# Parameter arithmetic queued where its inputs are ready, squares and PSUM evacuations with priority, in a one-core decoder layer

## The chip, the cores and the metric

The kernel runs on one core of one Trainium2 chip. The metric is the device time of one execution in microseconds (us), lower being better. A profile of one execution shows the engines of that core: PE (TensorE, the matrix engine), DVE (VectorE), ACT (ScalarE), POOL (GpSimd) and SP (SyncE, which here only issues DMAs). Each engine works through a queue of its own in a fixed order; an instruction that waits holds up everything behind it in its queue.

## The reference

One layer of a hybrid decoder, on 256 prompt tokens and 8 x 8 sample tokens (320 token columns in all):

```
h    = rms_norm(x, norm_mix)
proj = h @ w_in                        # split into S5 input u and retention q, k, v, g
S5:  dt = exp(log_step); lam_bar = exp(lam*dt); b_bar = (lam_bar - 1)/lam * b
     x_t = lam_bar * x_(t-1) + b_bar u_t;  y = Re(C x) + d*u;  gelu, sigmoid GLU
retention, 8 heads: rotary(q), rotary(k); masked decayed q k^T v + q R; group norm; silu(g)*o
x = x + concat(s5, ret) @ w_out
x = x + (silu(gate) * up) @ w_ffn_out,  gate, up = rms_norm(x, norm_ffn) @ w_ffn_in
```

The S5 states (64 groups of 64 complex numbers) and the retention states (8 heads of 128 x 128) are outputs too, and a final rms_norm gives y.

## The kernel before

Activations lie transposed, as 128 channels x 320 tokens. Every float32 matrix is split into a rounded high part and a remainder, so each 128 x 128 weight tile takes three matmuls of 320 columns: hi by x-hi, hi by x-lo, lo by x-hi (lines 141 to 143). Weights come in pieces of 8 tiles: SP loads `raw`, ACT casts it to `hi` (L130), DVE subtracts to get `lo` (L131); there are three buffers of each.

The input projection begins with four column blocks at once (two of u, head 0's q and k; L886), accumulated while x and these weights arrive step by step. Beside that, `split_x` makes the parts of x, and `square_x` squares x in place on ACT (L277) and adds the squares up on DVE into `u32[:, 0]`; the last of these additions gives the sum of squares for the norm. Then come, in PE's order: head 0's v (`ps_pv`), within it the column sums of the squares (`ps_r<-ones,u`) and the broadcast of 1/rms (`ps_r<-ident,ry`), then head 0's gate g, a u block, head 1's q, k and v, and so on. Small matmuls of the heads and of the S5 chunks are put between the GEMM steps by a clock of the program's own (`clk`, `spawn`, `run_due` with the delays `DL`): transposes `pst`, `pst2` (printed as `pst`), scores `pss`, outputs `po` and `psr`, `pn`, and for S5 `pt`, `pb`, `pk_`, `py`.

Two PSUM tags matter here. `acc` has two buffers, which the GEMM blocks take in turn: a block can start only when the block two before it has been read out. `misc` has two buffers, shared by `ps_pv`, `ps_r`, `pst`, `pss`, `pst2`, `psr`, `pn`, `pt` and `pk_`.

`s5_exps` computes dt and the decay `rr` on POOL (two calls of `vexp`, 23 small operations each) from the parameters `prm`, which a DMA brings. `s5_params` then works on DVE: angles `ang` = prm x dt, sines and cosines by polynomials into `ecs`, from them (and rr) the powers `lp`, the factor `ff` and the products `gp`, and `r4`, the fourth power of rr. `s5_turns` (POOL) makes tables `e18` (printed as `e`) from `ecs`; ACT copies `lp`, `ff`, `gp` into the layouts `lpc` and `gpc` (L475 to L478), which the chunks' products need, and `r4` into `d` (L590).

PE's and POOL's queues keep the order in which the program is written (`manual_schedule`), and SP's does for the first loads. All other queues are ordered by a scheduler that takes, of what it believes ready, the instruction with the highest priority; without a mark, what is written earlier goes first, and `tc.high_priority(offset=n)` moves instructions n places ahead (`EVAC` = 1500). `tc.issue_after(ins)` puts the instructions of its block behind `ins` on the same engine; it adds no wait between engines.

Of the kernel before, what the change touches and what calls it, by code (L numbers as in the profile page):

```python
# [44 lines left out]
def hybrid_kernel(ctx, tc, xT, w_in, w_in4, w_out, w_glu, w_fi, w_fo, vecs, s5p, bc, x0,  # L45
# [295 lines left out]
    def vexp(out, x, shape):  # L341
# [22 lines left out]
        pool.tensor_copy(ni, n)  # L364
        ptt(out, q, ni.bitcast(F32), MUL)

    sh = [P, NPAIR]
    she = [P, 3, NPAIR]
    shx = [P, NPAIR, NB]
# [7 lines left out]
        vexp(rr, lr, sh)  # L377
        return dt_, scr[1]

    def s5_params(dt_, used):  # L380
        newscr(0)

        ang = T(she)
        tt(ang[:, 0], prm[:, 1], dt_, MUL)
        ts(ang[:, 1], ang[:, 0], 8.0, MUL)
        ts(ang[:, 2], ang[:, 0], 64.0, MUL)
        nn = ts(T(she), ang, float(1 / np.pi), MUL, MAGIC, ADD)
        ts(nn, nn, MAGIC, SUB)
        for part in PI_PARTS:
            stt(ang, nn, -part, ang, MUL, ADD)  # L390
        par = ts(T(she), nn, 0.5, MUL, MAGIC, ADD)
        ts(par, par, MAGIC, SUB)
        stt(par, nn, 0.5, par, MUL, SUB)
        tt(par, par, par, MUL)
        ts(par, par, -8.0, MUL, 1.0, ADD)
        a2 = tt(T(she), ang, ang, MUL)
        ec, es = ecs[:, 0:NE], ecs[:, NE:]
        q = T(she)
        ts(q, a2, 1.0 / factorial(13), MUL, -1.0 / factorial(11), ADD)
        for kk in (9, 7, 5, 3, 1):  # L400
            tt(q, q, a2, MUL)
            ts(q, q, (1.0 if (kk // 2) % 2 == 0 else -1.0) / factorial(kk), ADD)
        tt(q, q, ang, MUL)
        tt(es[:, 0::3], q, par, MUL)
        q = T(she)
        ts(q, a2, -1.0 / factorial(14), MUL, 1.0 / factorial(12), ADD)
        for kk in (10, 8, 6, 4, 2, 0):
            tt(q, q, a2, MUL)
            ts(q, q, (1.0 if (kk // 2) % 2 == 0 else -1.0) / factorial(kk), ADD)
        tt(ec[:, 0::3], q, par, MUL)  # L410
        for l in range(2):
            n = (NE - 1 - l + 2) // 3
            c_, s_ = ec[:, l::3][:, :n], es[:, l::3][:, :n]
            u1, u2 = T([P, n, NPAIR]), T([P, n, NPAIR])
            tt(u1, c_, c_, MUL)
            tt(u2, s_, s_, MUL)
            tt(ec[:, l + 1::3][:, :n], u1, u2, SUB)
            stt(es[:, l + 1::3][:, :n], c_, 2.0, s_, MUL, MUL)
        s5_turns(ec, es)
        newscr(1)  # L420
        scr[1] = used
        tt(lp[:, 0, 0], rr, ec[:, 0], MUL)
        tt(lp[:, 1, 0], rr, es[:, 0], MUL)
        den = tt(T(sh), prm[:, 0], prm[:, 0], MUL)
# [12 lines left out]
        tt(ff[:, 1], t3, rden, MUL)
        r2 = tt(T(sh), rr, rr, MUL)
        tt(r4, r2, r2, MUL)

        def cmul(o, a, b, shape, tt=tt):

            u1, u2 = T(shape), T(shape)
            tt(u1, a[0], b[0], MUL)
            tt(u2, a[1], b[1], MUL)
            tt(o[0], u1, u2, SUB)
            tt(u1, a[0], b[1], MUL)
            tt(u2, a[1], b[0], MUL)
# [12 lines left out]
        def b8(a):
            return a.unsqueeze(2).to_broadcast(shx)

        def first_states():

            yield max(0.0, T0 + 1.0 - clk.now)
            newscr(0)
            cmul((lx0[:, 0], lx0[:, 1]), (x0t[:, 0], x0t[:, 1]), (b8(lp[:, 0, 3]), b8(lp[:, 1, 3])), shx,
                 pool.tensor_tensor)

        spawn(first_states())
        for q in range(2):
            for d in range(2):
                o = lpc[:, :, q, 4 * d:4 * d + 4]
                act.mul(o, lp[:, q].rearrange("p e (c j) -> p c j e", j=4), -1.0 if d > q else 1.0)  # L475
                o = gpc[:, :, q, 4 * d:4 * d + 4]
                act.copy(o[:, :, :, 0], ff[:, q].rearrange("p (c j) -> p c j", j=4))
                act.copy(o[:, :, :, 1:], gp[:, q].rearrange("p e (c j) -> p c j e", j=4))  # L478
# [90 lines left out]
    def s5_chunk(c):  # L569
# [42 lines left out]
        pt = misc("pt")  # L612
        for i in range(4):
            tr(pt[:, P * i:P * i + P], bl[:, i // 2, i % 2].rearrange("p u e h -> p (u e h)"))
        act.copy(bst, pt.rearrange("p (i s) -> p i s", s=P))

        for g in range(2):
            for d in range(CH):
# [12 lines left out]
        for i in range(2):  # L631
            for q in range(2):
                for u in range(2):
                    mm(0.04, pk_[64 * u:64 * u + 64, 32 * i:32 * i + 32],
                       bl[:, q, i, u].rearrange("p e h -> p (e h)"), cl[:, q, 2 * u + i, 0],
                       start=q == 0, stop=q == 1, tile_position=(0, 64 * u))
        for u in range(2):
            for g in range(2):
                hs = slice(16 * g, 16 * g + 16)
                act.copy(kbd[64 * g:64 * g + 64, 2 * u:2 * u + 2, hs],  # L640
                         pk_[64 * u:64 * u + 64, 0:64].rearrange("p (i h) -> p i h", h=32)[:, :, hs])
        with tc.high_priority(offset=2 * EVAC if c == 7 else 0):
            s5_scan(c, pb, xp, d0, tbl)
        yield DL["scan"]
# [44 lines left out]
    def head_k(h, q_, qg, k_, R):  # L689
# [2 lines left out]
        for i, s in enumerate(STARTS):  # L692
            tr(pst[:, P * i:P * i + P], k_[:, s:s + P])
        kd = mp.tile([P, 2, P], F32, name="kd", tag="kd", bufs=1)
        for i in range(2):
            act.mul(kd[:, i], pst[:, P * i:P * i + P], kdc[:, h, i:i + 1])
        act.mul(kv[64:128, h], pst[64:128, 2 * P:3 * P], kdc[64:128, h, 2:3])
        pss = misc("pss")
        mm(0.43, pss[:, 0:256], k_[:, 0:P], q_[:, 0:256], start=True, stop=True)
        mm(0.22, pss[:, 256:384], k_[:, P:256], q_[:, P:256], start=True, stop=True)  # L700
# [10 lines left out]
    def head_v(h, v_, qg, rt, R):  # L711
# [2 lines left out]
        for i, s in enumerate(STARTS):  # L714
            tr(pst2[:, P * i:P * i + P], v_[:, s:s + P])
        vT = mp.tile([P, 3, P], F32, name="vT", tag="vT", bufs=1)
        for i in range(3):
            act.mul(vT[:, i], pst2[:, P * i:P * i + P], rtok[:, i:i + 1])
        act.copy(kv[0:64, h], vT[64:128, 2])
        yield DL["o"]  # L720
        kd, sm = R["kd"], R["sm"]
# [28 lines left out]
        pool.tensor_tensor(y_, y_, w_, MUL)  # L750
        pool.tensor_tensor(w_, m_, y_, MUL)
        on = mp.tile([P, 4, P], F32, name="on", tag="on", bufs=1)
        for i in range(4):
            act.activation(on[:, i], po[:, i], AF.Identity, scale=y[:, 0, i:i + 1],
                           bias=y[:, 1, i:i + 1])
        psr = misc("psr")
        mm(0.22, psr[:, :P], kd[:, 0], vT[:, 0], start=True, stop=False)
        mm(0.22, psr[:, :P], kd[:, 1], vT[:, 1], start=False, stop=True)
        rp = mp.tile([P, P], F32, name="rp", tag="rp", bufs=1)
        act.copy(rp, psr[:, :P])  # L760
        sp.dma_start(rp_o[h], rp)
        yield DL["c"]
        pn = misc("pn")
# [98 lines left out]
    accs = [py0[:, :N], pb0[:, 0, :N], pb0[:, 1, :N], pk0[:, :N]]  # L862
    with tc.high_priority(offset=100000), tc.manual_schedule(engines={mybir.EngineType.SP}):
        act.dma_start(vec, vecs)
    k0 = 0
    for k1 in (1, *range(2, KT + 1, 2)):
        with tc.high_priority(offset=100000), tc.manual_schedule(engines={mybir.EngineType.SP}):
            if k0 % 2 == 0:
                raw, hi, lo = (wp.tile([P, 8, P], d, name=n, tag=n, bufs=3).rearrange("p (k o) m -> p k o m", o=4)
                               for n, d in (("raw", F32), ("hi", F32R), ("lo", F32R)))  # L870
            q = slice(k0 % 2, (k1 - 1) % 2 + 1)
            sp.dma_start(xrs[k0 // 4][:, k0 % 4:(k1 - 1) % 4 + 1], xT[:, k0:k1])
            sp.dma_start(raw[:, q], w_in4[:, k0:k1])
            if k1 == 6:
                sp.dma_start(prm, s5p)
            split_x(k0, k1)
            act.copy(hi[:, q], raw[:, q])
            dve.tensor_tensor(lo[:, q], raw[:, q], f(hi[:, q]), SUB)
        if k1 == 6:
            exps = s5_exps()  # L880
        if k1 % 2 == 0:
            accq = square_x(k1 - 2, k1)
        for k in range(k0, k1):
            for w_, x_ in ((hi, xhi), (hi, xlo), (lo, xhi)):
                for i, ps in enumerate(accs):
                    pe.matmul(ps, w_[:, k % 2, i], x_[:, k], start=k == 0 and w_ is hi and x_ is xhi,  # L886
                              stop=k == KT - 1 and w_ is lo)
            clk.now += 1.6
        k0 = k1
# [3 lines left out]
        sp.dma_start(t_, s_)  # L893
    for c in range(2):
        load_bc(c)
    s5_params(*exps)
    ytok = []
    rg = rstd_bcast(s5, accq, misc, "n1", ytok=ytok)

    def finish_norm():  # L900
# [4 lines left out]
        with tc.high_priority(offset=EVAC):  # L905
            act.copy(rbc, rps)
            tt(csr[:, 0], csr[:, 0], rbc, MUL)
            tt(csr[:, 1], csr[:, 1], rbc, MUL)
            tt(u32[:, 0], ps0, rbc, MUL)
            tt(u32[:, 1], ps1, rbc, MUL)  # L910
        rot_t["ready"] = True

    spawn(finish_norm(), DL["nm"])

# [356 lines left out]
```

## Time and profile before

| | us |
|---|---|
| median of 3 runs | 1465.54 (1464.16 to 1467.28) |
| profiled execution, device time | 1465.23 |
| its span, first to last instruction | 1463.2 |
| PE busy in the span | 1437.4 (98%) |
| DVE / ACT / POOL busy | 854.0 / 607.7 / 74.3 |
| mean granted TensorE clock | 0.994 of full speed |

2.0 us of the device time lie outside the span. A row of the timeline gives the start, the duration, engine, line, operation, output <- inputs and shapes, and in brackets how long the engine stood idle before the instruction and what it waited for.

### The profile page before, as it was taken

Reading aid. Unit: us, or ns where it says so; the run is one execution under the profiler, and the core shown is the slowest. Engines: PE = TensorE matmul, PEld = TensorE weight load, DVE = VectorE, ACT = ScalarE, POOL = GpSimd, SP = SyncE. Lnnn points to the kernel's source line nnn. Section 1 sums busy time; section 2 is a strip of 40 time slices with the busy share of each in tenths; the row PEclk is TensorE's granted clock in tenths of the full one; section 3 lists DMA queues with packets and bytes.
Section 4 is the critical chain, followed back from the end, with each engine's and each line's share of the span. In section 5 each row is a group of like instructions: output and inputs, shape, how many; then the busy total and the mean of one; then the engine's idle time right before and its main releaser. Section 6 shows DMA issues by size and latency. Waiting matters only on the chain.

```text
span 1463.2 us, 26296 instructions
## 1 busy us (share of the span) xinstructions
PE 1437.4 (98%) x10654; PEld 1422.6 (97%) x10654; DVE 854.0 (58%) x1402; ACT 607.7 (42%) x973; POOL 74.3 (5%) x163
## 2 busy tenths in 40 slices
PE   8799999999999999999999999999999999999997
PEld 8699999999999999999999999999999999999996
DVE  6878787778656755655444444444444444444454
ACT  6545555555345543333333333333333333333452
POOL 7321000000000000000000000000000000000001
PEclk9899999999999999999999999999999999999998
DMA  7355545554644485665444445444445544444443
GB/s 268 126 166 164 160 149 161 159 154 144 225 145 155 147 248 185 215 205 177 152 147 154 118 156 174 146 156 146 132 139 162 168 149 147 147 132 146 153 145 111
DMA packets 84712, 235.38 MB, mean 161 GB/s; under 512 B 16368, under 2 KB 32368, under 8 KB 84592
## 3 DMA queue, kind: packets, MB, share of 16 engines
q1 hardware_dynamic: 83680, 231.58, 49.6%
q10 hardware_dynamic: 912, 2.14, 0.5%
q8 instruction: 84, 1.38, 0.4%
q14 instruction: 36, 0.29, 0.1%
HBM read 222.63 MB, written 8.95 MB: 158 GB/s over the span
## 4 chain that ended last, share of the span: by engine, by line
PE 70%; DVE 0%; ACT 0%; DVEq 0%; issue 0%
PE ps_fg L141 7%; PE ps_fo L143 7%; PE ps_fo L142 7%; PE ps_fu L143 7%; PE ps_fg L143 7%; PE ps_fu L142 7%; PE ps_fg L142 7%; PE ps_fu L141 7%; PE ps_fo L141 7%; PE ps_o L143 1%; PE ps_o L141 1%; PE ps_o L142 1%; PE ps_g L142 1%; PE ps_g L143 1%; PE ps_g L141 1%; DVE x L176 0%
## 5 line engine op out<-in xcount | busy, mean ns | idle before, releaser
L131 DVE TENSOR_TENSOR lo<-raw,hi 128x1024 fp32r<-128x1024 f32 (+1 forms) x416 | 467.3, 1124 | 384.2 <-ACT hi L130 383.7
L130 ACT CAST hi<-raw 128x1024 fp32r<-128x1024 f32 (+1 forms) x416 | 402.2, 967 | 677.6 <-PE ps_fo L142 189.2
L141 PE MATMUL ps_fo<-ahi,hi 128*128 128x320 f32 x704 | 217.6, 309 | 0.0
L142 PE MATMUL ps_fo<-alo,hi 128*128 128x320 f32 x704 | 217.6, 309 | 0.0
L143 PE MATMUL ps_fo<-ahi,lo 128*128 128x320 f32 x704 | 217.6, 309 | 0.0
L141 PE MATMUL ps_fg<-hhi,hi 128*128 128x320 f32 x704 | 217.6, 309 | 0.0
L142 PE MATMUL ps_fu<-hlo,hi 128*128 128x320 f32 x704 | 217.4, 309 | 0.0
L142 PE MATMUL ps_fg<-hlo,hi 128*128 128x320 f32 x704 | 217.4, 309 | 0.0
L143 PE MATMUL ps_fu<-hhi,lo 128*128 128x320 f32 x704 | 217.4, 309 | 0.0
L143 PE MATMUL ps_fg<-hhi,lo 128*128 128x320 f32 x704 | 217.4, 309 | 0.0
L141 PE MATMUL ps_fu<-hhi,hi 128*128 128x320 f32 x704 | 217.4, 309 | 0.0
L141 PE MATMUL ps_p<-xhi,hi 128*128 128x320 f32 x560 | 178.1, 318 | 2.0 <-DVE k__776 L176 2.0
L143 PE MATMUL ps_p<-xhi,lo 128*128 128x320 f32 x560 | 173.7, 310 | 0.0
L142 PE MATMUL ps_p<-xlo,hi 128*128 128x320 f32 x560 | 173.6, 310 | 0.0
L142 PEld LDWEIGHTS ps_fg<-hlo,hi 128*128 128x128 f32 x704 | 132.4, 188 | 0.4
L141 PEld LDWEIGHTS ps_fg<-hhi,hi 128*128 128x128 f32 x704 | 132.4, 188 | 0.3
L141 PEld LDWEIGHTS ps_fu<-hhi,hi 128*128 128x128 f32 x704 | 132.4, 188 | 0.0
L143 PEld LDWEIGHTS ps_fg<-hhi,lo 128*128 128x128 f32 x704 | 132.4, 188 | 0.0
L142 PEld LDWEIGHTS ps_fu<-hlo,hi 128*128 128x128 f32 x704 | 132.4, 188 | 0.0
L143 PEld LDWEIGHTS ps_fu<-hhi,lo 128*128 128x128 f32 x704 | 132.4, 188 | 0.0
L141 PEld LDWEIGHTS ps_fo<-ahi,hi 128*128 128x128 f32 x704 | 132.2, 188 | 0.0
L142 PEld LDWEIGHTS ps_fo<-alo,hi 128*128 128x128 f32 x704 | 132.1, 188 | 0.0
(419 smaller groups left out, 1939.0 us busy)
## 6 DMA issues: line engine op xcount, KB each, us to landing
raw<-w_fi SPq DMA_DIRECT2D x176, 512.0 KB, 3.7
raw<-w_in SPq DMA_DIRECT2D x79, 512.0 KB, 4.1
raw<-w_fo SPq DMA_DIRECT2D x64, 512.0 KB, 3.5
raw<-w_out SPq DMA_DIRECT2D x32, 512.0 KB, 3.7
raw<-w_fo SPq DMA_DIRECT2D x64, 192.0 KB, 2.4
rt<-r SPq DMA_DIRECT2D x8, 512.0 KB, 5.4
raw<-w_glu SPq DMA_DIRECT2D x8, 512.0 KB, 3.6
raw<-r SPq DMA_DIRECT2D x8, 512.0 KB, 4.4
```

Source lines behind the costliest of these rows:

```text
L130: act.copy(hi[:, :m], raw[:, :m])
L131: dve.tensor_tensor(lo[:, :m], raw[:, :m], f(hi[:, :m]), SUB)
L141: pe.matmul(ps, hi, xhi[:, k], start=k == 0, stop=False)
L142: pe.matmul(ps, hi, xlo[:, k], start=False, stop=False)
L143: pe.matmul(ps, lo, xhi[:, k], start=False, stop=k == nk - 1)
```

## The change

Four things are edited. (1) `s5_params` is cut in two: its first half (angles, sines and cosines, turns) stays where it was written but is queued on DVE behind the fifth `lo` subtraction of the first loop; the second half, `s5_params2` (everything that needs rr, and den, r2, r4, ff, lp, gp), is written after the norm's evacuations and queued on DVE behind the second rotary factor `csr[:, 1]`. (2) The load of `prm` and with it the exponentials on POOL are issued one step of the loop earlier (k1 == 4, not 6). (3) `square_x` gets priority 50000. (4) The evacuations of `misc` and `po` PSUM that had no priority get `EVAC`: `bst`, `kbd`, `kd`, `kv`, `vT`, `on`, `rp`.

```diff
-    def s5_params(dt_, used):
+    def s5_params(dt_):
         newscr(0)
         ang = T(she)
...
         s5_turns(ec, es)
+
+    def s5_params2(used):
         newscr(1)
         scr[1] = used
         tt(lp[:, 0, 0], rr, ec[:, 0], MUL)
...
-        act.copy(bst, pt.rearrange("p (i s) -> p i s", s=P))
+        with tc.high_priority(offset=EVAC):
+            act.copy(bst, pt.rearrange("p (i s) -> p i s", s=P))
...
+        with tc.high_priority(offset=EVAC):
+            for i in range(2):
+                act.mul(kd[:, i], pst[:, P * i:P * i + P], kdc[:, h, i:i + 1])
+            act.mul(kv[64:128, h], pst[64:128, 2 * P:3 * P], kdc[64:128, h, 2:3])
...
-        for i in range(3):
-            act.mul(vT[:, i], pst2[:, P * i:P * i + P], rtok[:, i:i + 1])
+        with tc.high_priority(offset=EVAC):
+            for i in range(3):
+                act.mul(vT[:, i], pst2[:, P * i:P * i + P], rtok[:, i:i + 1])
         act.copy(kv[0:64, h], vT[64:128, 2])
...
-            if k1 == 6:
+            if k1 == 4:
                 sp.dma_start(prm, s5p)
...
-            dve.tensor_tensor(lo[:, q], raw[:, q], f(hi[:, q]), SUB)
-        if k1 == 6:
+            los.append(dve.tensor_tensor(lo[:, q], raw[:, q], f(hi[:, q]), SUB))
+        if k1 == 4:
             exps = s5_exps()
         if k1 % 2 == 0:
-            accq = square_x(k1 - 2, k1)
+            with tc.high_priority(offset=50000):
+                accq = square_x(k1 - 2, k1)
...
-    s5_params(*exps)
+    with tc.issue_after(los[4].ins):
+        s5_params(exps[0])
...
-            tt(csr[:, 1], csr[:, 1], rbc, MUL)
+            turned = dve.tensor_tensor(csr[:, 1], csr[:, 1], rbc, MUL)
...
         rot_t["ready"] = True
+
+        with tc.issue_after(turned.ins):
+            s5_params2(exps[1])
```

`kbd`, `on` and `rp` are marked like `bst`. PE's and POOL's queues hold the same instructions in the same order before and after. On ACT the squares stand in the same places as before, too. What moves stands on DVE, ACT and SP, and three places are shown.

DVE, around the last additions of the squares (`u_116` is `u32`; `scrt` is the scratch of the S5 parameters; `scrt<-rr` is the square of rr, `scrt<-prm,scrt` the angle). Before:

```order
L131 TENSOR_TENSOR lo<-raw,hi 128x1024
L176 TENSOR_TENSOR u_116<-u_116,retp 128x640
L176 TENSOR_TENSOR scrt<-prm,scrt 128x32
L176 TENSOR_TENSOR scrt<-rr 128x32
L176 TENSOR_TENSOR u_116<-u_116,retp 128x640
L170 TENSOR_SCALAR scrt<-scrt 128x32 x2
L176 TENSOR_TENSOR u_116<-u_116 128x320
```

After:

```order
L131 TENSOR_TENSOR lo<-raw,hi 128x1024
L176 TENSOR_TENSOR u_116<-u_116,retp 128x640
L176 TENSOR_TENSOR scrt<-prm,scrt 128x32
L176 TENSOR_TENSOR u_116<-u_116,retp 128x640
L170 TENSOR_SCALAR scrt<-scrt 128x32 x2
L176 TENSOR_TENSOR u_116<-u_116 128x320
```

The square of rr has left this place; it now stands behind the rotary factors, with the rest of `s5_params2`.

ACT, head 0's evacuations among the copies of the S5 parameters (`kd`, `kv` read `pst`; `vT` reads `pst2`, printed `pst_893`). Before:

```order
L843 ACTIVATE sg<-sg 128x320
L477 COPY gpc<-ff 128x8x4 x4
L696 ACTIVATE kd<-pst,kdc 128x128 x2
L475 ACTIVATE lpc<-lp 128x8x16 x2
L697 ACTIVATE kv<-pst,kdc 64x128
L718 ACTIVATE vT<-pst_893,rtok 128x128
L475 ACTIVATE lpc<-lp 128x8x16 x2
L718 ACTIVATE vT<-pst_893,rtok 128x128
L130 CAST hi<-raw 128x1024
L478 COPY gpc<-gp 128x8x4x3 x4
L718 ACTIVATE vT<-pst_893,rtok 128x128
```

After:

```order
L851 ACTIVATE sg<-sg 128x320
L701 ACTIVATE kd<-pst,kdc 128x128 x2
L702 ACTIVATE kv<-pst,kdc 64x128
L479 COPY gpc<-ff 128x8x4 x4
L592 COPY d_133<-r_123 128x8x63
L724 ACTIVATE vT<-pst_893,rtok 128x128 x2
L130 CAST hi<-raw 128x1024
L724 ACTIVATE vT<-pst_893,rtok 128x128
L477 ACTIVATE lpc<-lp 128x8x16 x4
L725 COPY kv<-vT 64x128
L592 COPY d_134<-r_123 128x8x63
L480 COPY gpc<-gp 128x8x4x3 x4
```

`kd` and `kv` stand ahead of all parameter copies now; `vT` stands behind the copies of ff and a copy of r4, which stood far earlier before.

DVE, the scan of a later S5 chunk beside the gelu of the chunk before it (`y`, then `u_116<-y`, which ends it). Before:

```order
L176 TENSOR_TENSOR t_3285<-pb,tb 128x2x128 x2
L176 TENSOR_TENSOR y_3071<-y_3071,y_3070 128x320
L176 TENSOR_TENSOR ends<-pb,lx_130 128x2x16
L176 TENSOR_TENSOR w<-t_3284,t_3285 128x256 x2
L180 SCALAR_TENSOR_TENSOR u_116<-y_3071,y_3070 128x320
L176 TENSOR_TENSOR ends<-pb,lx_130 128x2x16
L557 SCALAR_TENSOR_TENSOR w<-d_133,w 128x512
L176 TENSOR_TENSOR v_3299<-w,tb 128x512
L131 TENSOR_TENSOR lo<-raw,hi 128x1024
```

After:

```order
L176 TENSOR_TENSOR t_3285<-pb,tb 128x2x128 x2
L176 TENSOR_TENSOR ends<-pb,lx_130 128x2x16
L176 TENSOR_TENSOR w<-t_3284,t_3285 128x256 x2
L559 SCALAR_TENSOR_TENSOR w<-d_133,w 128x512
L176 TENSOR_TENSOR y_3071<-y_3071,y_3070 128x320
L176 TENSOR_TENSOR ends<-pb,lx_130 128x2x16
L176 TENSOR_TENSOR v_3299<-w,tb 128x512
L176 TENSOR_TENSOR v_3300<-w,tb 128x512
L131 TENSOR_TENSOR lo<-raw,hi 128x1024
L180 SCALAR_TENSOR_TENSOR u_116<-y_3071,y_3070 128x320
```

The two gelu operations stand behind the scan now, the last of them behind the next `lo` too.

More of the change, by code (lines that the diff above doesn't have):

```diff
@@ L365, in vexp @@
         ptt(out, q, ni.bitcast(F32), MUL)
+    ec, es = ecs[:, 0:NE], ecs[:, NE:]
     sh = [P, NPAIR]
@@ L396, in s5_params @@
         a2 = tt(T(she), ang, ang, MUL)
-        ec, es = ecs[:, 0:NE], ecs[:, NE:]
         q = T(she)
@@ L636, in s5_chunk @@
                        start=q == 0, stop=q == 1, tile_position=(0, 64 * u))
[L637 to L641, printed above, removed]
+        with tc.high_priority(offset=EVAC):
+            for u in range(2):
+                for g in range(2):
+                    hs = slice(16 * g, 16 * g + 16)
+                    act.copy(kbd[64 * g:64 * g + 64, 2 * u:2 * u + 2, hs],
+                             pk_[64 * u:64 * u + 64, 0:64].rearrange("p (i h) -> p i h", h=32)[:, :, hs])
         with tc.high_priority(offset=2 * EVAC if c == 7 else 0):
@@ L694, in head_k @@
         kd = mp.tile([P, 2, P], F32, name="kd", tag="kd", bufs=1)
-        for i in range(2):
-            act.mul(kd[:, i], pst[:, P * i:P * i + P], kdc[:, h, i:i + 1])
-        act.mul(kv[64:128, h], pst[64:128, 2 * P:3 * P], kdc[64:128, h, 2:3])
+        with tc.high_priority(offset=EVAC):
+            for i in range(2):
+                act.mul(kd[:, i], pst[:, P * i:P * i + P], kdc[:, h, i:i + 1])
+            act.mul(kv[64:128, h], pst[64:128, 2 * P:3 * P], kdc[64:128, h, 2:3])
         pss = misc("pss")
@@ L716, in head_v @@
         vT = mp.tile([P, 3, P], F32, name="vT", tag="vT", bufs=1)
-        for i in range(3):
-            act.mul(vT[:, i], pst2[:, P * i:P * i + P], rtok[:, i:i + 1])
+        with tc.high_priority(offset=EVAC):
+            for i in range(3):
+                act.mul(vT[:, i], pst2[:, P * i:P * i + P], rtok[:, i:i + 1])
         act.copy(kv[0:64, h], vT[64:128, 2])
@@ L752, in head_v @@
         on = mp.tile([P, 4, P], F32, name="on", tag="on", bufs=1)
-        for i in range(4):
-            act.activation(on[:, i], po[:, i], AF.Identity, scale=y[:, 0, i:i + 1],
-                           bias=y[:, 1, i:i + 1])
+        with tc.high_priority(offset=EVAC):
+            for i in range(4):
+                act.activation(on[:, i], po[:, i], AF.Identity, scale=y[:, 0, i:i + 1],
+                               bias=y[:, 1, i:i + 1])
         psr = misc("psr")
@@ L759, in head_v @@
         rp = mp.tile([P, P], F32, name="rp", tag="rp", bufs=1)
-        act.copy(rp, psr[:, :P])
+        with tc.high_priority(offset=EVAC):
+            act.copy(rp, psr[:, :P])
         sp.dma_start(rp_o[h], rp)
@@ L864, in hybrid_kernel @@
         act.dma_start(vec, vecs)
-    k0 = 0
+    k0, los = 0, []
     for k1 in (1, *range(2, KT + 1, 2)):
```

## The prediction

> **What bounds the kernel now.** I read the page's busy shares first (PE 98%), then the busy time of the engines by stretches, where each row gives the stretch, its length and the busy time of PE, weight loads, DVE, ACT and POOL, the granted clock and the DMAs; then PE's waits, and the timeline around each of them.
>
> ```profile
> 36.98:92.00 55.02, 44.06 (x295) 43.28 (x296) 47.33 (x149) 25.92 (x58) 21.57 (x43) 0.91 0.44 136
> 92.00:430.00 338.00, 338.00 (x3202) 327.90 (x3200) 251.34 (x507) 174.10 (x378) 19.97 (x56) 1.00 0.53 164
> ```
>
> PE bounds it. From 92 to 430 us it is never idle (338.00 of 338.00), so an edit to the later heads and S5 chunks has nothing to win there. Everything that can be won lies between 36.98 and 92 us, where PE lacks 10.96 us and its granted clock is 0.91 of full. Three waits make up the lack:
>
> ```profile
> 36.66 0.31 PE L143 MATMUL ps_pv<-xhi,lo 128*128 128x320 f32 x1
> 40.60 0.83 PE L102 MATMUL ps_r<-ones,u 128*128 128x1 f32 x6 [3.62 <-DVE u L176]
> 41.53 0.47 PE L142 MATMUL ps_pv<-xlo,hi 128*128 128x320 f32 x1
> 41.80 0.47 PE L143 MATMUL ps_pv<-xhi,lo 128*128 128x320 f32 x1
> 44.96 0.31 PE L143 MATMUL ps_pv<-xhi,lo 128*128 128x320 f32 x1
> 48.18 0.83 PE L102 MATMUL ps_r<-ident,ry 128*128 128x128 f32 x6
> 58.95 0.41 PE L141 MATMUL ps_p<-xhi,hi 128*128 128x320 f32 x1 [2.02 <-DVE k__776 L176]
> 61.69 0.49 PE L107 MATMUL pst<-ident,k__776 128*128 128x128 f32 x3
> 68.33 0.90 PE L107 MATMUL pst<-ident,v__780 128*128 128x128 f32 x3 [5.32 <-ACT kv L697]
> 72.22 0.30 PE L141 MATMUL ps_p<-xhi,hi 128*128 128x320 f32 x1
> 73.09 0.83 PE L102 MATMUL po<-vT,sm 128*128 128x128 f32 x6
> 86.43 0.60 PE L107 MATMUL pn<-ident,on 128*128 128x128 f32 x4
> 91.70 0.31 PE L141 MATMUL ps_p<-xhi,hi 128*128 128x320 f32 x1
> ```
>
> Matmuls of 320 columns follow each other by 0.147 us (six from 72.22 to 73.09), but by 0.267 us (41.53, 41.80) after the waits of 3.62 and 5.32 us, until 44.96 and 72.22; after that of 2.02 us they don't slow. The first wait thus costs 3.62 us and 1.61 us (fourteen matmuls in the 3.67 us up to 44.96, less 14 x 0.147), the second 2.02, the third 5.32 and 1.58 (twelve matmuls in the 3.34 us up to 72.22, less 12 x 0.147). I call them A (5.23), B (2.02), C (6.90): together 14.15 us.
>
> **A.** What did the sum of squares wait for? DVE's and POOL's queues tell:
>
> ```profile
> 31.58 0.19 DVE L176 TENSOR_TENSOR scrt<-prm,scrt 128x32 f32<-128x32 f32 x1
> 39.05 0.19 DVE L176 TENSOR_TENSOR scrt<-rr 128x32 f32<-128x32 f32 x1 [7.28 <-POOL rr L365]
> 40.06 0.48 DVE L176 TENSOR_TENSOR u<-u 128x320 f32<-128x320 f32 x1
> 32.03 1.05 ACT L130 CAST hi<-raw 128x1024 fp32r<-128x1024 f32 x1 [1.99 <-PE ps_p L886]
> 41.71 0.33 SPq L129 DMA_DIRECT2D raw<-w_in  x1
> ```
>
> DVE stood 7.28 us before the square of rr, with two additions behind it. In the new order that square is gone from there: 31.7 plus 0.75 + 0.2 + 0.4 gives the sum at 33.1, while PE comes to `ps_r` at 36.98. A goes entirely. What is late next? `lo` follows (the cast of 32.03 ends at 33.08 as before), frees a `raw` buffer, and SP's load of 41.71 goes out at 34.4, and with it the `raw_bc` load behind it that ACT's `cl` copies need. DVE then waits 0.3 us for the third cast (PE frees its buffer at 36.1) and runs the rsqrt by 40.7, before PE's next need: the broadcast, which stood 7.58 us behind the column sums (40.60 to 48.18) and, without the slow pitch, comes 5.97 us behind them, at 43.0. The earlier `prm` load puts one 48 KB transfer ahead of x and weights that PE needs over 1 us after their landing: nothing, within 0.3 us either way. The priority on the squares moves none of them on ACT: nothing.
>
> **B.** The evacuation of that broadcast, the rotary factors that need it, and the rotation of k that empties the `acc` buffer PE waited for:
>
> ```profile
> 49.27 0.42 ACT L906 COPY rbc<-ps_r 128x320 f32<-128x320 f32 x1
> 52.28 0.88 DVE L176 TENSOR_TENSOR csr<-csr,rbc 128x320 f32<-128x320 f32 x2
> 58.41 0.48 DVE L176 TENSOR_TENSOR k__776<-ps_p,csr 128x320 f32<-128x320 f32 x1
> ```
>
> `rbc` ended 1.51 us behind the broadcast's start, so now at 44.5. DVE's factors lagged it by 2.6 us, behind a `lo` and twelve parameter operations; now that `lo` runs at 41.8 and nine operations end by 44.5, so the factors come at 44.5, 7.8 us earlier, while PE is 5.2 ahead. From there ACT sets the pace: a cast, v's and u's copies, two `sw` copies, a cast whose buffer PE frees at 48.4 and two `sw` copies more end at 50.5; DVE's `lo` of that last cast ends at 51.3, and `k_` reads its PSUM to 51.75. PE, 8.6 us behind the broadcast as before (its matmul before the wait ended at 56.93, its next would have started at 56.8), arrives at 51.6. B shrinks to 0.15: 1.87 gained, and PE is 7.1 us ahead.
>
> **C.** The rows of ACT, DVE and POOL at the third wait:
>
> ```profile
> 64.39 0.37 ACT L477 COPY gpc<-ff 128x32 f32<-128x32 f32 x2 [3.47 <-DVE ff L176]
> 65.19 0.62 ACT L696 ACTIVATE kd<-pst,kdc 128x128 f32<-128x128 f32 x2
> 67.91 0.36 ACT L697 ACTIVATE kv<-pst,kdc 64x128 f32<-64x128 f32 x1
> 61.29 1.55 DVE L131 TENSOR_TENSOR lo<-raw,hi 128x1024 fp32r<-128x1024 f32 x1
> 71.68 1.23 DVE L131 TENSOR_TENSOR lo<-raw,hi 128x1024 fp32r<-128x1024 f32 x1 [1.12 <-ACT hi L130]
> 62.76 0.52 DVE L176 TENSOR_TENSOR scrt<-scrt,prm 128x32 f32<-128x32 f32 x2
> 65.52 0.18 DVE L176 TENSOR_TENSOR lp<-scrt 128x32 f32<-128x32 f32 x1
> 67.66 0.61 DVE L176 TENSOR_TENSOR sm<-pss,mk 128x256 f32<-128x256 f32 x2
> 59.50 0.51 POOL L490 COPY e<-ecs 128x64 f32<-128x64 f32 x1 [20.22 <-DVE ecs L176]
> 69.63 0.34 POOL L508 TENSOR_TENSOR ta<-e 128x32 f32<-128x32 f32 x1
> ```
>
> ACT waited 3.47 us for ff with `kd` behind, and then for lp with `kv` behind (between 65.81 and 67.91). Both now stand ahead: `pst` at 54.6 (61.69 less 7.1), `kd` half a microsecond later, `kv` done 0.62 + 0.36 after that, at 56.1; PE is there at 55.9 (68.33 less 5.32 less 7.1). 0.25 us is left, and the clock stays: 6.65 gained.
>
> **D, a new wait.** `vT` now stands behind the copies of ff and r4, and `sm` on DVE behind most of the second half. DVE starts on that half at 53.5: four small operations (0.6), a `lo` (1.5), then 16 small ones. Between 62.76 and 65.70, beside POOL's turns (59.50 to 69.97), eleven such took 2.95, 0.27 each; the turns need ecs, so they now run 50.2 to 60.7, beside these again. ff comes at 57.9 and 59.0, r4 between, `sm` from 60.2. ACT: copies of ff to 59.4, of r4 to 60.0, `vT` twice to 60.65, a cast, the third `vT` at 62.05. PE arrives at `po` 3.2 us behind `pst2` (73.09 - 68.33 less 1.58), at 59.35, starts at 60.75, waits for the third `vT` to 62.1: D costs 2.1. Its bounds are 0 (pitch 0.15, as after 69.6) and 5.5 (below).
>
> **E and F, the chain behind it.** PE is now 11.65 us ahead; the S5 chain isn't:
>
> ```profile
> 76.61 0.31 POOL L744 TENSOR_SCALAR mv<-mv 128x4 f32<-128x4 f32 x1 [6.22 <-DVE mv L741]
> 81.46 1.50 ACT L754 ACTIVATE on<-po,gy 128x128 f32<-128x128 f32 x4 [3.18 <-POOL gy L751]
> 83.93 1.65 DVE L131 TENSOR_TENSOR lo<-raw,hi 128x1024 fp32r<-128x1024 f32 x1 [1.45 <-ACT hi L130]
> 89.28 0.48 DVE L176 TENSOR_TENSOR q__1095<-ps_p,csr 128x320 f32<-128x320 f32 x1
> ```
>
> Head 1's v (PE 91.70) needs the buffer that `q__1095` empties at 89.76, 1.9 us before. The chain to it is: the rest of lp and gp with a `lo` (DVE to 65.6), `gpc`, a product, the statistics to 68.5, POOL's eight steps (4.85), `on` (1.5, to 74.85; PE needs it from 74.8: no wait), the cast behind it (1.05), `lo` (1.65, to 77.55), one `cl` and four `e` products, the table (3.6 where 2.2 of it stood behind before), a `lo`, the rotation: done at 82.75. F: PE wants that first `lo` at 76.8 and waits 0.75. E: PE arrives for v at 91.70 - 11.65 + 0.75 = 80.8 and waits 2.0. Their bounds are none and 6.6 together (lock-out, below); I take the count, since each row of it is one of before.
>
> Sum: -5.23 - 1.87 - 6.65 + 2.1 + 0.75 + 2.0 = -8.9. From the profiled 1465.23 that is 1456.3; the median of the runs lies 0.3 higher, so I say 1456.5. Behind 92 us the queues keep their slack, less 2 us.
>
> **A rule against it.** POOL's turns now overlap the second half of the parameters. The row: the same `lo` takes 1.55 beside them, 1.23 without, a slowing by a quarter. The Trainium skill (SBUF — State Buffer, Who interferes with whom) says that a DVE instruction with two SBUF inputs and a GpSimd one that reads SBUF lock each other out entirely. By that rule the small operations would each wait out a POOL operation, and D and E would grow; the trace of before shows a good deal less than that.
>
> **The rivals.**
> No new waits: if the scheduler's order leaves D alone or nothing (DVE pitch 0.15, E absent), -13.75 to -11.65: 1451.5 to 1453.6. For it: DVE has 4.0 us of waits between 52 and 89 to give back. Against: the chain above is counted row by row.
> Lock-out (the rule above, priced by rows): POOL's turns take 10.5 us for 25 operations, 0.42 each; 16 small operations at 0.14 + 0.42 instead of 0.27 are 4.6 us later, `sm` at 64.8, D at 5.5 with half clock behind it, and the chain's end at 87.4, which is what counts: -4.3, 1460.9.
> Given back: the chain ends as late as before, at 89.8, and PE waits for it: no change, 1465. Against: the factors alone are 7.8 us earlier and only some 2 us of work is added behind them.
> Slower: in the later chunks the last gelu operation stands behind the scan, two products and a `lo` (1.2 + 1.3 + 1.2), some 3 us later. The `kst` loads wait for it in SP's queue, and weight loads stand behind them:
>
> ```profile
> 251.04 0.49 DVE L180 SCALAR_TENSOR_TENSOR u<-y,y 128x320 f32<-128x320 f32 x1
> 251.97 0.32 SPq L582 DMA_DIRECT2D kst<-via  x1
> 255.05 0.33 SPq L129 DMA_DIRECT2D raw<-w_in  x1
> ```
>
> The load behind comes 3 us later anyway, so it decides only if the operation moves by over 3 us plus the weights' own lead; four chunks at over 3 us each would eat the 8.9 and 2.9 more: 1468.5 or above.
>
> **How the numbers follow.** Forecast (D, E, F about as counted, 1454.5 to 1459): 0.52. No new waits: 0.18. Lock-out or a longer chain, 1459 to 1462.5: 0.20. Given back, within 0.2% (2.9 us, about what the runs can tell): 0.06. Slower: 0.04. Range 1452.5 to 1461.5: it leaves out the last two and the ends of the second and third. Faster 0.90, same 0.06, slower 0.04.
>
> **What would show it.** Right: no wait at `ps_r` and no 0.267 us pitch after it; `u<-u` ends near 33; `rbc` near 44; `pst` for v without a long wait; a wait of 1 to 3 us at `po` on sm or vT, and one at head 1's v on `q__1095`; 92 to 430 still full. Wrong: a wait over 3.6 us anywhere with the slow pitch behind it, DVE's small operations at 0.5 us beside POOL, or PE waiting on `lo` or `hi` after 90 us.

## The result and the profile after

The changed kernel takes 1455.76 us (median of 4 runs, 1454.40 to 1456.62) against 1465.91 (median of 4 runs of the kernel before, 1464.16 to 1467.28, taken beside them): a ratio of 0.9931, 95% interval 0.9913 to 0.9948. The forecast was 1456.5, range 1452.5 to 1461.5. The profiled execution took 1454.40 us, its span 1452.3, so it stands 10.9 us below the span before; it is the fastest of its four runs, and part of why is in the last section.

First the same two stretches of the changed kernel as were shown of the kernel before (start and end, length, busy time of PE, weight loads, DVE, ACT, POOL, clock, DMAs):

```profile
36.98:92.00 55.02, 51.05 (x362) 49.50 (x361) 47.46 (x140) 29.85 (x64) 22.57 (x43) 1.00 0.52 164
92.00:430.00 338.00, 337.67 (x3196) 327.39 (x3195) 251.12 (x508) 174.88 (x377) 22.03 (x56) 1.00 0.52 162
```

PE is busy for 51.05 us of the first stretch instead of 44.06, at full clock instead of 0.91. In the second it was full before and lacks 0.33 us now. PE's waits (total, times, longest):

```profile
PE po L102 <- DVE sm L176: 1.8, 1, 1.8
PE ps_p L141 <- DVE q__1095 L176: 1.4, 1, 1.4
PE py L895 <- ACT hi L885: 1.1, 2, 0.7
...
PE ps_p L141 <- DVE k__776 L176: 0.5, 1, 0.5
...
PE pst L107 <- ACT kv L702: 0.3, 1, 0.3
```

The wait of 3.62 us is gone, that of 5.32 has shrunk to 0.3, that of 2.02 to 0.5, and the first two at `po` and `q__1095` are new. PE's timeline at the same places, and ahead of `ps_r` the last addition that gives the sum:

```profile
31.35 0.48 DVE L176 TENSOR_TENSOR u<-u 128x320 f32<-128x320 f32 x1
35.60 0.72 PE L102 MATMUL ps_r<-ones,u 128*128 128x1 f32 x6
41.55 0.83 PE L102 MATMUL ps_r<-ident,ry 128*128 128x128 f32 x6
50.78 0.42 PE L141 MATMUL ps_p<-xhi,hi 128*128 128x320 f32 x1 [0.48 <-DVE k__776 L176]
55.11 0.55 PE L107 MATMUL pst<-ident,v__780 128*128 128x128 f32 x3 [0.27 <-ACT kv L702]
60.13 0.91 PE L102 MATMUL po<-vT,sm 128*128 128x128 f32 x6 [1.83 <-DVE sm L176]
73.60 0.60 PE L107 MATMUL pn<-ident,on 128*128 128x128 f32 x4
80.62 0.42 PE L141 MATMUL ps_p<-xhi,hi 128*128 128x320 f32 x1 [1.38 <-DVE q__1095 L176]
84.70 0.60 PE L107 MATMUL pt<-ident,bl 128*128 128x128 f32 x4
```

Against 40.60, 48.18, 58.95, 68.33, 73.09, 86.43 and 91.70 before, PE is ahead by 5.00, 6.63, 8.17, 13.22, 12.96, 12.83 and 11.08 us; `pt`, at 95.66 before, by 10.96, and so it stays to the end (10.9). In this execution 1.38 us of the lead were there ahead of all this, since PE came to `ps_r` at 35.60 us against 36.98; 1.21 of them arose where the third group of matmuls of the first loop starts, at 9.89 us against 11.10.

### The profile page after: what moved, and what is told of

It is laid out like the page before. It is cut to its first block, busy times and chain, and to the rows that moved or that the text cites. A ratio compares the mean times of both kernels' runs of the same rounds, so it can differ in the third digit from the quotient of the medians.

```text
span 1452.3 us, 26302 instructions
## 1 busy us (share of the span) xinstructions
PE 1435.0 (99%) x10654; PEld 1419.5 (98%) x10654; DVE 852.8 (59%) x1402; ACT 607.5 (42%) x973; POOL 80.7 (6%) x163
## 3 DMA queue, kind: packets, MB, share of 16 engines
q8 instruction: 84, 1.38, 0.4%
## 4 chain that ended last, share of the span: by engine, by line
PE 70%; DVE 1%; ACT 0%; issue 0%; DVEq 0%
PE ps_fo L142 7%; PE ps_fu L141 7%; PE ps_fo L141 7%; PE ps_fu L142 7%; PE ps_fu L143 7%; PE ps_fo L143 7%; PE ps_fg L141 7%; PE ps_fg L142 7%; PE ps_fg L143 7%; PE ps_o L141 1%; PE ps_o L142 1%; PE ps_o L143 1%; PE ps_g L142 1%; PE ps_g L143 1%; PE ps_g L141 1%; DVE x L176 0%
```

## The experiments

Line numbers in rows of an experiment are its own. Since the start of the program varies between executions, the table has, beside the medians, what depends on it least: the stretch from PE's coming to `ps_r` (its start less its wait) to `pt`, the four transposes of `bl` in head 1's v. The columns from the first matmul on are of one profiled execution each.

| kernel | median us (runs) | ratio to before, 95% | first matmul | at `ps_r` | `pt` | stretch |
|---|---|---|---|---|---|---|
| before | 1465.91 (4) | | 4.74 | 36.98 | 95.66 | 58.68 |
| changed | 1455.76 (4) | 0.9913 to 0.9948 | 4.74 | 35.60 | 84.70 | 49.10 |
| 1 split only | 1456.46 (5) | 0.9926 to 0.9953 | 4.74 | 35.94 | 87.42 | 51.48 |
| 2 priorities only | 1461.35 (7) | 0.9961 to 0.9982 | 4.78 | 38.25 | 91.66 | 53.41 |
| 3 `prm` late | 1455.87 (5) | 0.9922 to 0.9947 | 4.75 | 36.77 | 85.24 | 48.47 |
| 4 early priorities only | 1457.23 (5) | 0.9929 to 0.9954 | 8.06 | 39.21 | 87.49 | 48.28 |
| 5 turns late | 1456.72 (5) | 0.9923 to 0.9948 | 8.06 | 38.70 | 87.08 | 48.38 |
| 6 table late | 1455.68 (5) | 0.9918 to 0.9943 | 8.06 | 39.55 | 86.13 | 46.58 |
| 7 both | 1455.19 (5) | 0.9911 to 0.9938 | 8.05 | 39.61 | 86.30 | 46.69 |
| 8 changed, again | 1456.50 (5) | 0.9925 to 0.9950 | 8.05 | 38.70 | 86.93 | 48.23 |
| 9 zeroing late | 1454.88 (5) | 0.9913 to 0.9938 | 4.70 | 37.78 | 86.14 | 48.36 |
| 10 before, zeroing late | 1466.81 (11) | 0.9997 to 1.0015 | 4.75 | 44.38 | 97.25 | 52.87 |
| 11 zeroing and `prm` late | 1456.53 (5) | 0.9922 to 0.9946 | 4.73 | 36.28 | 87.32 | 51.04 |
| 12 both, zeroing late | 1453.00 (4) | 0.9901 to 0.9928 | 4.70 | 35.99 | 82.85 | 46.86 |

Runs 1 to 4, 5 to 8 and 9 to 12 each ran together on one chip, the kernel before among them (1465.73, 1465.26 and 1465.98). The two profiles of the changed kernel, with the first matmul at 4.74 and at 8.05 us, have spans of 1452.3 and 1454.4. Which start the executions had that were only timed isn't known, so a difference of 1 us or so between two medians isn't put down to an edit unless the profiles show where it arises.

**1. The split alone.** All six new priorities taken out again, such as

```diff
-        with tc.high_priority(offset=EVAC):
-            for i in range(2):
-                act.mul(kd[:, i], pst[:, P * i:P * i + P], kdc[:, h, i:i + 1])
-            act.mul(kv[64:128, h], pst[64:128, 2 * P:3 * P], kdc[64:128, h, 2:3])
+        for i in range(2):
+            act.mul(kd[:, i], pst[:, P * i:P * i + P], kdc[:, h, i:i + 1])
+        act.mul(kv[64:128, h], pst[64:128, 2 * P:3 * P], kdc[64:128, h, 2:3])
```

> The changed kernel without its six new priorities: the split of the parameters, the earlier prm load and the squares stay. If the split alone pays A and B, and the priorities alone pay C: no wait at ps_r and none over 1 us at head 0's k rotation, but the second kd copy stands behind four copies of ff on ScalarE, which end near 59.5 us, so that PE waits some 4.4 us for kv (0.27 in the changed kernel) with slow pitch behind it; the new waits at po and at head 1's v are then covered. About 2.5 to 3 us above the changed kernel, 1458 to 1459. If the split alone pays for everything, since it takes the second half out of the way of the copies: no wait at kv, 1455.8.

PE's longest wait, and ACT's timeline around it:

```profile
PE pst L107 <- ACT kv L699: 4.2, 1, 4.2
```

```profile
58.23 0.36 ACT L479 COPY gpc<-ff 128x32 f32<-128x32 f32 x2 [0.50 <-DVE ff L176]
58.48 0.36 ACT L698 ACTIVATE kd<-pst,kdc 128x128 f32<-128x128 f32 x1
58.85 0.36 ACT L699 ACTIVATE kv<-pst,kdc 64x128 f32<-64x128 f32 x1
```

No wait at `ps_r`, 0.34 us at the k rotation, and 4.23 at kv, behind the copies of ff: A and B are the split's, C is mostly the priorities'. The stretch is 2.4 us longer than in the changed kernel, as expected. The runs show less of it: the median is 0.7 us above the changed kernel's, below the 1458 expected, and the two intervals overlap.

**2. The priorities alone**, on the kernel before.

> The kernel before with the six new priorities alone: nothing is split, moved or loaded earlier. If A needs the move of the square of rr, it stays whole here: the wait at ps_r of 3.6 us with slow pitch behind it, and B of 2.0. C shrinks, because kd now stands behind two copies of ff only and kv behind kd: its wait goes from 5.3 to about 2.8 us, without slow pitch, -2.5 to -4; part of it may come back at head 1's v, whose buffer came free only 1.9 us ahead of need. 1461.5 to 1463. If the priorities pay nothing without the split: within 1 us of the kernel before.

```profile
PE ps_r L102 <- DVE u L176: 2.5, 1, 2.5
PE ps_p L141 <- DVE k__776 L176: 2.1, 1, 2.1
...
PE pst L107 <- ACT kv L700: 1.2, 1, 1.2
```

The sum's matmul starts at 40.75 us (40.60 before), although PE came to it 1.27 us later: rr decides, not PE. B stays. kv is done at 65.88 instead of 68.27, and `pt` comes 4.0 us earlier than before; the medians differ by 4.4. So the priorities alone are worth 4.4 us, the split alone 9.3, and both together 10.2 in these medians: they don't add, since with either alone PE comes later to `po` and to head 1's v, where the new waits D and E then don't arise.

**3. `prm` loaded and the exponentials begun at the old place** (`k1 == 6`, not 4).

> The changed kernel with the prm load and the exponentials back at their old place (behind the fourth load of weights). PE's third group of matmuls started 1.2 us earlier in the profile of the changed kernel than in that before (9.89 against 11.10 us). If that is the landing of x and weights from one execution to another, as the prediction's 'nothing' for this edit has it: the same time as the changed kernel within 0.5 us, no wait at ps_r. If the earlier prm load brings it: 1.2 us slower, 1457, and the group starts near 11.1 again.

The median is the changed kernel's (1455.87), with no wait at `ps_r`. The third group did start late again, at 11.06 us. Run 11 is the second look at that.

**4. No priority on `bst`, `kbd`, `on` and `rp`.**

> The changed kernel without the priorities on bst, kbd, on and rp; kd, kv and vT keep theirs. If nothing behind 92 us is to be won, as PE is never idle there: the same as the changed kernel within 0.5 us, PE full from 92 to 430 us. If the priority on the later heads and chunks pays: 1 us or more slower than the changed kernel, with new waits of PE between 80 and 430 us.

From 92 to 430 us PE is busy for 337.66 of 338 us, no new wait stands behind 92 us, and the stretch is 48.28. By its median the run would fit the second half of its expectation, by its profile the first. The 1.5 us by which the median lies above the changed kernel's are inside the intervals, and the profile has 3.16 us of waiting at the first matmul, of which below. Nothing was found that these four priorities bring.

The square's priority was not run by itself: without it every engine's queue holds the same instructions in the same order, so it moves nothing.

**5. The turns late.**

```diff
-        s5_turns(ec, es)
...
-        tt(r4, r2, r2, MUL)
+        r4i = dve.tensor_tensor(r4, r2, r2, MUL)
+        with tc.issue_after(r4i.ins):
+            dve.tensor_copy(ecs, ecs)
+        s5_turns(ec, es)
```

> The changed kernel with GpSimd's turns held back until r4 is written (one copy of the factors onto themselves on VectorE stands between), so that the small operations ahead of sm run without GpSimd. In the changed kernel the operations between 54.5 and 59.5 us start 0.31 us apart on average. If GpSimd's turns slow them: they start 0.10 to 0.15 us apart, the second ff is done before 57 us, sm before PE comes to po, and the wait at po (1.83) falls to at most 1 us, now on vT. Since the turns then end near 67 us, the normalization on GpSimd starts no earlier than now, and head 1's v waits longer by what po gained: the same time as the changed kernel within 0.7 us. If the operations are slow by themselves: the same 0.31 us apart, the same wait at po.

In the changed kernel (first profile), the slow ones among DVE's small operations, and POOL's operations at the same time:

```profile
56.34 0.18 DVE L176 TENSOR_TENSOR scrt<-rr 128x32 f32<-128x32 f32 x1
56.44 0.72 DVE L176 TENSOR_TENSOR ff<-scrt 128x32 f32<-128x32 f32 x1
57.09 0.18 DVE L176 TENSOR_TENSOR scrt<-scrt 128x32 f32<-128x32 f32 x1
57.19 0.18 DVE L176 TENSOR_TENSOR r<-scrt 128x32 f32<-128x32 f32 x1
57.29 0.64 DVE L176 TENSOR_TENSOR scrt<-lp 128x32 f32<-128x32 f32 x1
57.85 0.18 DVE L176 TENSOR_TENSOR ff<-scrt 128x32 f32<-128x32 f32 x1
57.96 0.64 DVE L176 TENSOR_TENSOR scrt<-lp 128x32 f32<-128x32 f32 x1
```

```profile
56.34 0.77 POOL L499 TENSOR_TENSOR e<-e,ta 128x256 f32<-128x256 f32 x1
57.19 0.69 POOL L500 TENSOR_TENSOR ta<-e,ecs 128x256 f32<-128x256 f32 x1
57.84 0.70 POOL L501 TENSOR_TENSOR e<-e,ecs 128x256 f32<-128x256 f32 x1
```

The three slow ones end at 57.16, 57.93 and 58.60, each 0.05 to 0.06 us behind the end of a POOL operation (57.11, 57.88, 58.54); the others start 0.10 us apart. With the turns late, the same operations:

```profile
55.81 0.18 DVE L176 TENSOR_TENSOR scrt<-scrt 128x32 f32<-128x32 f32 x1
56.62 0.18 DVE L176 TENSOR_TENSOR ff<-scrt 128x32 f32<-128x32 f32 x1
57.26 0.18 DVE L176 TENSOR_TENSOR ff<-scrt 128x32 f32<-128x32 f32 x1
57.57 0.61 DVE L176 TENSOR_TENSOR sm<-pss,mk 128x256 f32<-128x256 f32 x2
```

From the operation at 55.81 to the end of the second ff, 11 operations take 1.30 us (1.63 less 0.33 for the copy among them), 0.12 each; in the changed kernel the same 11 took 2.93 (from 54.54 to 58.03, less 0.56 for the `scrt<-lp` of 57.29, which comes later here), 0.27 each. `sm` is early, and the wait at `po` is gone entirely. But the stretch is 48.38, as long as in run 8 beside it (48.23), because the waits came back behind it:

```profile
PE ps_p L141 <- DVE q__1096 L176: 1.6, 1, 1.6
...
PE pn L107 <- ACT on L763: 0.7, 1, 0.7
...
PE ps_p L143 <- DVE lo L131: 0.3, 1, 0.3
```

This is the chain that the prediction followed to E and F: turns that start later end later (68.4 us, against 63.4 in run 8), now beside the second part of DVE's small operations, and `on` comes at 74.16 us, no earlier than in run 8 (74.19).

**6. The table late**: chunk 0's six table operations behind the first product of head 1's q rotation.

```diff
-        tbl = s5_table(c)
+        if c:
+            tbl = s5_table(c)
         yield DL["b1"] + (4.0 if c == 0 else 0.0)
+        if c == 0:
+            with tc.issue_after(rot_t["rots"][2].ins):
+                tbl = s5_table(c)
```

> The changed kernel with chunk 0's table (four products e, two combinations tb) queued on VectorE behind the first product of head 1's q rotation instead of ahead of it; nothing else moves there. If the wait E at head 1's v is the table's place in the queue: the rotation starts near 78.5 instead of 80.1 us, the wait of 1.38 us is gone, 1.4 us faster than the changed kernel, 1454.4. If the weight cast and lo ahead of the rotation set it: 0.3 us or less gained. If the table is then late for the scan or lo for PE: a new wait of PE behind 85 us takes it back.

In the changed kernel the table (`e`, `tb`) and a `lo` stand between chunk 0's last `cl` and the rotation that PE waits for from 79.24 us on:

```profile
76.58 1.79 DVE L176 TENSOR_TENSOR e<-e 128x256 f32<-128x256 f32 x4
78.28 0.75 DVE L176 TENSOR_TENSOR tb<-e,e 128x256 f32<-128x256 f32 x2
80.09 0.48 DVE L176 TENSOR_TENSOR q__1095<-ps_p,csr 128x320 f32<-128x320 f32 x1
```

With the table late the same operation is done at 81.64 us, before PE comes to head 1's v at 82.17:

```profile
79.59 1.65 DVE L131 TENSOR_TENSOR lo<-raw,hi 128x1024 fp32r<-128x1024 f32 x1
81.16 0.48 DVE L692 TENSOR_TENSOR q__1086<-ps_p,csr 128x320 f32<-128x320 f32 x1
```

The wait at head 1's v is gone and none comes in its place: the stretch is 46.58, 1.65 us shorter than in run 8. The median is 0.8 us lower, which the runs can't tell from nothing. E was the table's place in DVE's queue.

**7. Both**: the table late, and of the turns the last level and what follows it behind r4.

> The changed kernel with the table late as in the run before, and of GpSimd's turns only the last level and what follows it held back until r4 is written, so that GpSimd is free before the normalization of head 0. If D is the small operations beside GpSimd and E the table's place: the wait at po falls from 1.83 to about 1 us and that at head 1's v is gone, 2.2 us faster than the changed kernel, 1453.6. If D stays: 1454.4.

PE's waits behind `ps_r`, all of them up to the later stages:

```profile
PE pn L107 <- ACT on L772: 0.5, 1, 0.5
...
PE ps_p L143 <- DVE lo L131: 0.3, 1, 0.3
PE pst L107 <- ACT kv L713: 0.3, 1, 0.3
```

D and E are gone, and PE then runs into `on`: the list has only the wait of 0.49 us for the first of its four parts, but the transposes `pn` that read them follow 0.35 us apart instead of 0.11, which is 0.7 us more. The stretch is 46.69, no better than with the table alone. Half of the expectation (D pays another 0.8) failed: without D, PE is early for the next link of the same chain.

**8. The changed kernel again.**

> The changed kernel again, beside the three others on the same chip, and for a second profile. If the start of PE's third group of matmuls (9.89 us in the first profile, 11.06 with a late prm load) varies from execution to execution: it lies anywhere between 9.7 and 11.2 us, and the waits at po and at head 1's v are 1.83 and 1.38 us again. If the half clock behind a wait goes by the wait's length alone: none behind the 1.83 us at po, as before.

The waits at `po` and at head 1's v are 1.72 and 1.38 us. The third group doesn't tell, since the first matmul already came 3.3 us late. Its wait of 3.15 us is for DVE's first `xhi`, and that ends at 7.91, 0.18 us behind POOL's zeroing of S5 tiles:

```profile
3.36 4.54 DVE L170 TENSOR_SCALAR xhi<-u,vec 128x320 fp32r<-128x320 f32 x1 [3.36 <-DMA vec<-vecs]
```

```profile
5.46 2.26 POOL L324 MEMSET cl<- 128x1280 f32 x2
```

**9 to 12. The zeroing late.** The memsets (POOL, 2.1 to 7.7 us) go between the two exponentials.

```diff
-    for t_ in (*d0s, *xps, kbd, ush, *cls_):
-        pool.memset(t_, 0.0)
...
         pool.tensor_tensor(lr, prm[:, 0], dt_, MUL)
+        for t_ in (*xps, *cls_, *d0s, kbd, ush):
+            pool.memset(t_, 0.0)
         vexp(rr, lr, sh)
```

> The changed kernel with GpSimd's zeroing of eight S5 tiles (4.6 to 5.8 us of memsets back to back from 2.1 us on) moved into the gap between its two exponentials. In five of the profiles VectorE's first xhi took 4.5 us, from 3.4 to 7.9, up to the end of those memsets, and PE's first matmul came at 8.05; in the others 1.2 to 1.3 us and 4.74. If the memsets lock that operation out, and by chance in some executions: it takes under 0.6 us, the first matmul comes at 4.74 or before, the runs scatter by less than before (1454.4 to 1456.6) and lie near 1454 or below. rr is then written some 5 us later, near 44, which the split makes harmless: no wait at ps_r. If the late first matmul is the landing of a load: no change, 1456.

```profile
3.37 0.39 DVE L170 TENSOR_SCALAR xhi<-u,vec 128x320 fp32r<-128x320 f32 x1 [3.37 <-DMA vec<-vecs]
```

0.39 us in all four profiles with the zeroing late, and the first matmul at 4.70 to 4.75; 1.20 us or more in all ten with the zeroing early. That lock is shown. The gain in time is less clear: 1454.88, with the third group waiting 1.75 us and half clock behind it.

> The same move of the memsets in the kernel before, where the square of rr stands ahead of the additions for the sum of squares. If A is what the prediction says, the wait of the sum for rr: rr comes some 5 us later, the sum's matmul ps_r starts near 45 instead of 40.6 us, its wait grows from 3.6 to 7 or more, and the kernel is 3 to 5 us slower than the kernel before, 1469 to 1471, whatever the start gains. If the sum waits for something else: no slower than before.

Missed, and a kernel that doesn't test what it was meant to. With rr later by the scheduler's own reckoning, it put the square of rr behind the additions by itself: `u<-u` ends at 40.7, before rr (44.2), and there is no wait at `ps_r`. In its place the angle stands ahead of a `lo` on DVE and waits for dt:

```profile
21.36 0.19 DVE L176 TENSOR_TENSOR scrt<-prm,scrt 128x32 f32<-128x32 f32 x1 [5.65 <-POOL scrt L363]
```

```profile
24.36 0.63 PE L886 MATMUL py<-xhi,lo 128*128 128x320 f32 x1 [5.05 <-DVE lo L878]
```

So this kernel says the same of A from another side (without the square ahead of the additions, the sum doesn't wait for rr), and shows the same fault one place earlier, at 5.05 us instead of 3.62. It is no faster than the kernel before (ratio 1.0006).

> The changed kernel with the zeroing late and, as in the third run, the prm load back at its old place: with the start free of the memsets, the place of the prm load can be read from PE's third group of matmuls. In three profiles with a late prm load that group waited 1.9 us, in two with an early one 0.73. If the place decides it: the same here, 1.9 us, and 0.5 to 1.2 us slower than the same kernel with the early load. If it is chance: no such difference.

The third group started at 10.56, against 10.54 in run 9: with `xhi` free the place of the `prm` load makes no difference there. The 1.65 us between the medians, and 2.7 between the stretches, are elsewhere: a wait of 2.30 us at the k rotation. In this run the memsets, at their new place, caught DVE again. Two small operations, of 0.17 and 0.20 us in run 9, are held up, with the sum's last addition behind them, until the last memset ends (34.73 us):

```profile
31.79 2.99 DVE L170 TENSOR_SCALAR scrt<-scrt 128x32 f32<-128x32 f32 x2
33.56 1.17 POOL L377 MEMSET ush<- 128x1280 f32 x1
```

The sum is still in time for PE, but DVE's queue is some 2.3 us late, and the rotary factors start 2.6 us behind the end of `rbc` instead of 0.4 in run 9.

> The seventh run (table late, last level of the turns late) with the zeroing late as well. If the three gains add: 1.3 us below the changed kernel with the zeroing late, about 1452.5, and below the kernel before by 13 us. If the later rr or the memsets' new place collide with the turns or the rotation: no faster than the seventh run, 1455.

1453.00 us, the fastest kernel of the study: 12.98 us below the kernel before and 1.9 below run 9 beside it. Its interval, 0.9901 to 0.9928, still overlaps those of run 9 (0.9913 to 0.9938) and of the changed kernel (0.9913 to 0.9948); its stretch, 46.86, is 1.5 us below run 9's.

## Why the prediction was right, step by step

**A** (counted -5.23): -5.25 in the profile, from the lead of 6.63 us at the broadcast less the 1.38 that was there at `ps_r`. Run 2 keeps the wait with the square of rr left in place; runs 1 and 3 are without it, though the one lacks the priorities and the other the early `prm` load. Shown.

**B** (-1.87): -1.54. The k rotation was 0.48 us late, not 0.15; where PE itself came later (run 8), nothing was left of the wait.

**C** (-6.65): the wait fell by 5.05 us and the slow pitch of 1.58 is gone, -6.63. Runs 1 and 4 together show that the priority on kd and kv does it: without all six the wait is 4.23 us, with those of kd, kv and vT alone it is 0.27.

**D** (+2.1): 1.83 us of wait and 0.16 of a slower restart, 2.0. It stood for `sm`, one of the two named: 1.4 us had been counted for `sm` and 0.7 for the third `vT`, while `sm` alone took 1.83 and `vT` (done at 60.77) nothing, so that the sum came out this close is in part luck. The pitch behind it was counted as 0.27 us per small operation and was 0.27 over the eleven of run 5, 0.31 over the sixteen up to `sm`. The reason given for choosing it was wrong, though. The prediction held the lock-out rule against the slowing of one `lo` and concluded that the trace showed a good deal less than the rule. The rows of run 5 fit the rule instead: a DVE operation that is caught waits to the end of the POOL operation, and without POOL beside it none does. What the rival mispriced is how often: it let every DVE operation wait out a POOL operation, but in these rows one or two slip through behind the end of each POOL operation (57.09 and 57.19 above), so that there are no more waits than POOL has operations. The Trainium skill (SBUF — State Buffer, Who interferes with whom) has whoever issues first hold the shared pair of ports for the whole instruction while the other fully blocks; the ends 0.05 us apart agree with that.

**F** (+0.75): no wait, 0.2 us of pitch at that `lo`. **E** (+2.0): 1.38 us of wait, about 1.65 with the restarts. Run 6 puts E on the table in DVE's queue, as counted. F and D are links of one chain: take one away and the next shows (runs 5 and 7).

**The sum** (-8.9): in the stretch to which it applies, -9.6 in the first profile and -10.5 in the second. The terms A to D were right to 0.4 us each; the difference is F and E, counted 0.9 us too dear together, less the 0.3 us by which B was counted too high, and in the second profile B's wait of 0.48 us and its restart, which a later PE doesn't see.

**Nothing for the `prm` load**: the first profile's 1.21 us at the start was outside the bound of 0.3, but the times of runs 3 and 11 don't confirm a gain there. Profiles with the early load and a punctual first matmul have the third group at 9.89, 10.23, 10.54 and 10.28 us, those with the late load at 11.10, 10.94, 11.06, 10.75 and 10.56. A few tenths may be real; this stays open.

**Nothing for the squares and behind 92 us**: the squares' priority moves no row, and run 4 finds nothing for the rest. **The slower rival** (the `kst` loads in SP's queue) had no effect: the 0.33 us that PE lacks between 92 and 430 us is a wait for `ylo`, which the kernel before has just behind 430; no wait there is for weights.

## What to carry to other kernels

A small operation whose input comes late from another engine belongs behind everything on its queue that the bottleneck waits for; look for the queue's one long idle time and read what stands behind it, as the square of rr here or the angle in run 10. When a stall is taken away, follow the chain to its next link before adding up: D and E were there to be counted, and mending D alone paid nothing. And work that nobody waits for yet, such as zeroing tiles, may lock out an operation of another engine that is needed now; moving it only helps where nothing urgent stands beside its new place (run 11).

## What the runs showed of the hardware

**The start.** DVE's first `xhi`, a scalar operation over one tile, took 0.39 us in four profiles with no memset beside it. Beside POOL's memsets it took 1.20 to 1.31 us in five profiles and 4.51 to 4.62 in five others, and in all ten it ended 0.18 us behind the end of a memset: in the first five behind that which ends at 4.41 us, in the others behind the last. The same program thus starts at 4.74 or at 8.05 us. Of the first profiles, before and after both had the early start, so the comparison stands.

**Half clock behind a wait.** The prediction took the slow pitch to follow waits of 3.6 us and more, and not of 2.02. All waits of 3.62 us or more between dense matmuls had it (4.23, 5.05, 5.32, 6.15). Between 1.7 and 2.5 us the same length goes either way: none behind 1.83 us at `po` in the changed kernel, but half clock behind 1.82 at the same place in run 9. The 2 us that begin 2 us behind the start of `po`, in the changed kernel and in run 9 (the clock is the third number from the end):

```profile
62.13:64.13 2.00, 2.00 (x15) 2.00 (x16) 1.93 (x6) 1.98 (x7) 0.00 (x0) 1.00 0.02 4
```

```profile
63.55:65.55 2.00, 2.00 (x15) 1.68 (x8) 1.93 (x6) 1.98 (x7) 0.00 (x0) 0.50 0.01 4
```

Run 2 had it behind 2.11 and 2.50 us, run 11 not behind 2.30.

The traces show what decides. In every profile the granted clock changes only at times that lie whole multiples of 3.41 us apart (in the kernel before at 41.48, 44.90, 65.38 and 72.20 us), and where these times lie differs between executions of one program: by 1.0 us between the two profiles of the changed kernel. Between 1.7 and 2.5 us it mattered how this grid cut the wait. The 1.75 us of run 4, the 1.75 (third group) and 1.82 of run 9 and the 1.90 (third group) and 2.11 of run 2 fell whole into one stretch of 3.41 us, and the next stretch was at half clock. The 2.02 us of the kernel before were cut into 1.62 and 0.40, the 1.83 of the changed kernel into 0.65 and 1.19, the 2.30 of run 11 into 1.28 and 1.02, and no half clock followed. The bound isn't sharp: 1.72 us (run 8) and 1.77 (run 3) in one stretch had none, and the 2.50 us at `ps_r` in run 2 had it with 1.54 in one stretch, which also held the six one-column matmuls.

The Trainium skill (TensorE: Matmul & The Clock Gate, Part 1: The HAM clock gate) has the clock go by a window of about 3.4 us that runs freely, whatever the kernel does; that agrees with the grid of 3.41 us and with the same wait going both ways. It also puts half clock behind a whole idle window, and here 1.75 us in one window (run 4, at `po`) were enough. A wait of 2 us is therefore priced at 2 us or at some 3.6, and which one depends on how that execution's grid cuts it, which for the one who predicts is chance.
